# One row-block pair of the q and k projection computed with seven block products instead of eight

## The chip, the cores and the metric

The kernel runs on one core of a Trainium2 chip. The metric is the device time of one execution in microseconds (us); the time of a kernel is the median of its runs. Engines by their short names: PE is TensorE (matmuls; PEld its weight loads), DVE is VectorE, ACT is ScalarE, POOL is GpSimd, SP is SyncE, which here only issues DMAs.

## The reference, cut to what matters

One encoder layer of a hybrid model: 256 tokens, 2048 features, all in float32.

```python
hn = rms_norm(h, g_mix_pre[i])
u = hn @ w_in[i]                       # (256, 2048) @ (2048, 5120)
q, k, v, xr, yg = jnp.split(u, [D_ATTN, 2 * D_ATTN, 3 * D_ATTN, 3 * D_ATTN + D_REC], axis=-1)
attn = neighborhood_attention(q, k, v, rpb[i])
rec = rglru_bidirectional(xr, ...) * jax.nn.gelu(yg)
mixed = jnp.concatenate([rms_norm(attn, ...), rms_norm(rec, ...)], axis=-1) @ w_out[i]
h = h + rms_norm(mixed, g_mix_post[i])
...                                    # SwiGLU feed-forward network, then a gated embedding
```

The change is in `u = hn @ w_in`, the first large product. What follows it is the same work in both kernels.

## The kernel before

**Products.** Every large product is 256 tokens times a weight matrix. Weights come in tiles of 512 KB: two row blocks of 128 (a *row-block pair*) by 512 columns, f32. ACT rounds a tile to fp32r (`wh`, line 700), DVE takes the rest (`wl = w - wh`, line 716), and the features are split the same way (`hT_hi`, `hT_lo`, lines 331 and 333). A block product of 128 tokens by 128 rows by 512 columns is then three matmuls of 128x512: hi by hi, lo by hi, hi by lo. The third is the one that reads `wl`. A tile takes two token halves times two row blocks times three, 12 matmuls (`products`, line 758).

**Input projection.** The 5120 columns are ten chunks of 512, in the order `x0 v0 q0 k0 x1 q1 k1 v1 g0 g1`; each chunk has eight row-block pairs. The first two chunks take turns (`turns(first, hT, KS, apart=2)`): x0 and v0 alternate for six pairs, then x0 takes its last two, then v0. This stretch is the *head*; its sixteen tiles are called T0 to T15 here in the order in which PE takes them, so T8 is x0's fifth pair and T9 v0's fifth. From q0 on each chunk runs alone. During the head SP also fetches the transposed input `xs` (two halves of 1 MB; the last load of the second half is behind T9's) and, for the row norms, the input again as four loads `xn` of 512 KB, whose squares ACT sums. Only when these are there (`rstd_x`) can any chunk of the projection leave PSUM.

**A unit of seven.** The feed-forward part already uses, for some row-block pairs, a scheme of 2x2 blocks with seven products instead of eight: the two token halves by two row blocks on one side, the two row blocks by two column chunks on the other. Per pair it needs four sums of feature blocks (`sums_of`, S1, S2, S7, S4), sums of weight blocks (`sum_stream`: three additions of 128x512 on DVE, and one more that a DMA on POOL's queue makes by accumulating, `added`), and a combination of the accumulators in PSUM (`made_of_four`) before the rest of the pairs is added on top. PE does it in three steps: `four_products` (12 matmuls on two tiles, into four PSUM banks), later `two_products` (6) and `one_product` (3): 21 matmuls for two tiles instead of 24.

**What sets the order.** The program is built by a planner (`Plan`): each stream of work is a generator that names the engine, a cost and the slots it takes, and the planner fixes one order for each engine. On the chip each engine then takes its instructions in that order and waits for what is missing. Raw weight tiles have four buffers (`wr`), which the lo step (line 716) frees; split tiles four pairs (`wh`, `wl`); PSUM has eight banks, four called `acc` and four called `sm`. SP's loads stand in one order too: a load that waits for a buffer holds those behind it.

Of the kernel before, what the change touches and what calls it, by code (L numbers as in the profile page):

```python
# [44 lines left out]
PLE_KS = (0, 2)  # L45
BEGIN = (6, 7)
# [5 lines left out]
def seven_ks(f):  # L52
# [13 lines left out]
    (lambda c: (("w_ple_gate", c), ("w_ple_gate", c + 1)), (2,), PLE_KS),  # L66
]
# [187 lines left out]
def layer(ctx: ExitStack, tc: tile.TileContext, a: dict, out: bass.AP):  # L255
# [211 lines left out]
    class Group:  # L467
# [23 lines left out]
        def two(self, j):  # L491
            i = len(tiles)
            tiles.append(None)
            self.twos[j] = i
            lower[self.own[j] + 1] = -1
            segs.append((two_products, self, j, i))
# [77 lines left out]
    def load_stream():  # L574
        for i, tl in enumerate(tiles):
# [3 lines left out]
            w, k, n0 = tl  # L579
            if min(fours) <= i < i_ple:  # L580
# [40 lines left out]
    def sum_stream():  # L621

        for i in sorted(fours):
# [26 lines left out]
            done(ev_raw[two, 2])  # L650

# [54 lines left out]
    def lo_stream():  # L706
        last_one = max(f[1] for f in ffn_fours().values())
        for i in range(len(tiles)):
# [16 lines left out]
            if i in fours:  # L725
                plan.add(last_sum(i), plan.now, -2 * SOON)

# [74 lines left out]
    def made_of_four(group):  # L802
# [49 lines left out]
    def sums_of(lhs, kx, hi, lo):  # L852
# [7 lines left out]
        kind = "mid" if lhs is hP or kx == 6 else "T4"  # L860
        for j in range(2):
            h, l = lhs.at[kx + j]
            yield dve(S, take=None if j else kind)
            if not j and kind == "mid":
# [107 lines left out]
    for i in range(2 * NT):  # L972
        extra_loads.setdefault((10 + i, 0), []).append(load_xn(i))
# [75 lines left out]

    def open_p1():  # L1050
        t1["hs"], t1["rec_hi"] = big(0, "hs", F32), big(1, "rec_hi")
# [14 lines left out]
        for n in ("qh", "ql", "kh", "kl"):  # L1066
            t1[n] = p1.tile([P, HB, S], F32R, name=n)
        for n in ("vh", "vl"):
            t1[n] = p1.tile([P, NT, N], F32R, name=n)
        t1["pp"] = p1.tile([P, 2, NT, 2, KEYS], F32R, name="pp")  # L1070
# [6 lines left out]
        nc.gpsimd.memset(ssr, 0.0)  # L1077

# [20 lines left out]
    def second_tiles():  # L1099
        plan.reach(ev_x)  # L1100
        t1["rec_lo"], t1["attnT"] = big(2, "rec_lo"), big(3, "attnT", F32)
# [393 lines left out]
    first = []  # L1495
    for n, c in enumerate(ORDER.split()):
        (n0, post), half = CHUNKS[c[0]], int(c[1])
        ch = Chunk(post(half), (open_p1, second_tiles)[n] if n < 2 else None)
        if n < 2:
            first.append((ch, "w_in", n0 + half * N))  # L1500
        if n == 1:
            turns(first, hT, KS, apart=2)
        elif n > 1:
            seg(ch, "w_in", n0 + half * N, hT, KS, after=start_biases if n == 3 else None)
# [747 lines left out]
    for i in range(min(fours), max(f[1] for f in fours.values() if f[4] is hF.ev_sums)):  # L2252
        if i % (W_BUFS + MORE_W) < MORE_W:
            more_w[i] = i % (W_BUFS + MORE_W)
    places = list(RING)
    for n, i in enumerate(sorted(lower)):
        lower[i] = next(j for j in places if j < 3 or n < len(lower) - 4)
        places.remove(lower[i])
        places.append(lower[i])
    first_slot = {i: n % 2 for n, i in enumerate(sorted(fours))}  # L2260
# [147 lines left out]
```

## Time and profile before

| | us |
|---|---|
| median of 3 runs (1138.49 to 1139.64) | 1139.56 |
| the profiled execution, its time | 1138.81 |
| the profiled execution, its span | 1137.0 |
| PE busy | 1127.5 |
| DVE busy | 962.1 |
| ACT busy | 741.0 |
| POOL busy | 154.5 |

The span runs from the first to the last instruction; 1.81 us of the execution lie around it. Busy time of PE is of little use as a share: a matmul of 128x512 is booked with 390 ns, while the next starts 227 ns after it. What counts is whether PE ever waits, and that is read from the rows of its waits and from the starts of its weight loads. In the page's forty slices PE's granted clock stands at 9 (90% or more) throughout. The DMA engines move 237 GB/s on average over the span.

### The profile page before, as it was taken

The numbers are of one execution on the slowest core, as the hardware profiler recorded it, in microseconds if no ns is written. First come the engines' busy times: TensorE is split into PE (matmuls) and PEld (weight loads), VectorE is DVE, ScalarE is ACT, GpSimd is POOL, SyncE is SP. The second block draws the span as 40 slices with busy tenths as digits, with TensorE's granted clock in tenths as the row PEclk, the third lists the DMA queues.
The fourth block names the chain that finished last, engine by engine and source line by source line (L and its number), as shares of the span: only waits on it lengthen the run. The fifth ranks groups of instructions, "written<-read, shape, count | busy, mean of one in ns | idle before, by whom it ended". The sixth has DMA issues, their size and how long they took to land.

```text
span 1137.0 us, 15223 instructions
## 1 busy us (share of the span) xinstructions
PE 1127.5 (99%) x5140; PEld 938.2 (83%) x5140; DVE 962.1 (85%) x1250; ACT 741.0 (65%) x994; POOL 154.5 (14%) x245
## 2 busy tenths in 40 slices
PE   9999999999999999999999999999999999999997
PEld 8888888888888888888888888888888888888886
DVE  6768787788469998899998889999989988888986
ACT  6776788876448566566566656666565664676674
POOL 0000000000000032232011043132121223200200
PEclk9999999999999999999999999999999999999999
DMA  8867566565686986887887777897887788967862
GB/s 311 303 193 219 173 183 187 166 201 181 206 302 184 344 254 226 234 259 222 277 285 232 240 222 216 249 269 235 271 275 280 233 242 255 305 208 271 269 198 101
DMA packets 110686, 269.54 MB, mean 237 GB/s; under 512 B 36432, under 2 KB 42576, under 8 KB 109200
## 3 DMA queue, kind: packets, MB, share of 16 engines
q1 hardware_dynamic: 95568, 242.60, 64.0%
q0 software_dynamic: 14752, 25.84, 11.1%
q8 instruction: 40, 0.66, 0.2%
q14 instruction: 38, 0.31, 0.1%
q10 hardware_dynamic: 288, 0.14, 0.0%
HBM read 250.70 MB, written 9.44 MB: 229 GB/s over the span
## 4 chain that ended last, share of the span: by engine, by line
PE 96%; DVE 1%; ACT 1%; DMA 1%; issue 0%; SPq 0%; DVEq 0%; POOL 0%; ACTq 0%; POOLq 0%
PE acc L758 69%; PE acc L769 8%; PE acc L768 8%; PE acc L767 8%; PE tr L344 1%; DVE wl L716 0%; DMA sq<-ev 0%; PE half L2119 0%; PE acc L2119 0%; PE warm L2305 0%; PE pg L391 0%; PE pg L392 0%; PE pg L393 0%; ACT wh L700 0%; PE po L1435 0%
## 5 line engine op out<-in xcount | busy, mean ns | idle before, releaser
L716 DVE TENSOR_TENSOR wl<-wr,wh 128x1024 fp32r<-128x1024 f32 (+1 forms) x295 | 352.9, 1210 | 77.8 <-ACT wh L700 72.4
L700 ACT CAST wh<-wr 128x1024 fp32r<-128x1024 f32 (+1 forms) x295 | 304.9, 1042 | 136.8 <-PE acc L758 84.2
L758 PE MATMUL acc<-wh,hT_mix_hi 128*128 128x512 f32 x376 | 146.6, 390 | 0.0
L758 PE MATMUL acc<-wh,hT_mix_lo 128*128 128x512 f32 x376 | 146.3, 389 | 0.0
L758 PE MATMUL acc<-wl,hT_mix_hi 128*128 128x512 f32 x376 | 146.3, 389 | 0.0
L700 ACT CAST wh<-ple 128x1024 fp32r<-128x1024 f32 (+1 forms) x75 | 76.0, 1018 | 82.2 <-DVE ple L643 54.6
L363 POOL DMA_DIRECT2D mT<-mid x164 | 96.8, 636 | 238.3 <-DVE mid L353 117.6
L758 PE MATMUL acc<-wl,hT_hi 128*128 128x512 f32 x320 | 124.6, 390 | 0.0
L758 PE MATMUL acc<-wh,hT_hi 128*128 128x512 f32 x316 | 124.5, 394 | 0.0
L758 PE MATMUL acc<-wh,hT_lo 128*128 128x512 f32 x316 | 123.2, 390 | 0.0
L669 POOL DMA_DIRECT2D ple<-in_w_ffn_up x32 | 28.7, 897 | 539.7 <-DVE ple L643 386.3
L716 DVE TENSOR_TENSOR wl<-ple,wh 128x1024 fp32r<-128x1024 f32 (+1 forms) x75 | 88.0, 1177 | 9.3 <-ACT wh L700 9.3
L758 PEld LDWEIGHTS acc<-wl,hT_mix_hi 128*128 128x128 f32 x376 | 70.6, 188 | 14.7 <-DVE wl L716 0.2
L758 PEld LDWEIGHTS acc<-wh,hT_mix_hi 128*128 128x128 f32 x376 | 70.6, 188 | 14.6
L758 PEld LDWEIGHTS acc<-wh,hT_mix_lo 128*128 128x128 f32 x376 | 70.6, 188 | 14.6
L758 PEld LDWEIGHTS acc<-wl,hT_hi 128*128 128x128 f32 x320 | 60.1, 188 | 13.1 <-DVE wl L716 0.2
L758 PEld LDWEIGHTS acc<-wh,hT_lo 128*128 128x128 f32 x316 | 59.4, 188 | 11.6
L758 PEld LDWEIGHTS acc<-wh,hT_hi 128*128 128x128 f32 x316 | 59.4, 188 | 11.4
L758 PE MATMUL acc<-w,hT_mix_hi 128*128 128x512 f32 x144 | 47.3, 389 | 0.0
L716 DVE TENSOR_TENSOR wl<-lower,wh 128x1024 fp32r<-128x1024 f32 x35 | 42.4, 1215 | 3.1 <-ACT wh L700 3.1
L700 ACT CAST wh<-lower 128x1024 fp32r<-128x1024 f32 x35 | 36.6, 1052 | 10.7 <-PE acc L758 6.8
L758 PE MATMUL acc<-wh,hT_ffn_hi 128*128 128x512 f32 x96 | 37.8, 393 | 0.4 <-ACT hT_ffn_hi L331 0.4
(472 smaller groups left out, 2536.6 us busy)
## 6 DMA issues: line engine op xcount, KB each, us to landing
wr<-in_w_in SPq DMA_DIRECT2D x77, 512.0 KB, 4.5
wr<-in_w_ffn_gate SPq DMA_DIRECT2D x70, 512.0 KB, 5.6
wr<-in_w_ffn_down SPq DMA_DIRECT2D x54, 512.0 KB, 6.0
wr<-in_w_ffn_up SPq DMA_DIRECT2D x50, 512.0 KB, 5.0
wr<-in_w_out SPq DMA_DIRECT2D x32, 512.0 KB, 4.4
wr<-in_w_ple_gate SPq DMA_DIRECT2D x30, 512.0 KB, 4.7
lower<-in_w_ffn_up SPq DMA_DIRECT2D x27, 512.0 KB, 6.4
third<-in_w_ffn_gate SPq DMA_DIRECT2D x18, 512.0 KB, 5.7
```

Source lines behind the costliest of these rows:

```text
L344: nc.tensor.transpose(tr[:, b, t * P : (t + 1) * P], e[:, t, sl], ident)
L363: (nc.gpsimd if i in pool else nc.sync).dma_start(dst[32 * j : 32 * j + 32, :, :, i, :], src[32 * i : 32 * i + 32, :, :, j, :],)
L669: nc.gpsimd.dma_start(dst, src, accum_op=ALU.add)
L700: nc.scalar.copy(his[i][:, 0 : src.shape[1], :] if n == 2 else his[i][:, j, :], src)
L716: nc.vector.tensor_tensor(out=los[i][:, m, :], in0=src, in1=f32(his[i][:, m, :]), op=ALU.subtract)
L758: nc.tensor.matmul(accs[t], x[:, sl], w[:, j, :], start=st and m == 0, stop=sp and m == 2, **group)
L767: nc.tensor.matmul(dst, x[0], wh, start=start, stop=False, skip_group_check=seeded)
L768: nc.tensor.matmul(dst, x[1], wh, start=False, stop=False, skip_group_check=seeded)
L769: nc.tensor.matmul(dst, x[0], wl, start=False, stop=stop, skip_group_check=seeded)
```

## The change

One unit of seven is put into the input projection: row-block pair 0 of q0 and k0 (`IN_KS = (0,)`). Its `four_products` step is placed inside the head, after five turns of x0 and v0 (`IN_AT = (5,)`), that is between T9 and what was T10. Its two tiles Q and R are loaded there; Q takes a `wr` buffer, R a tile of its own. The `xn` loads move four tiles back (from tiles 10 to 13 to tiles 14 to 17 of the new count). x0 and v0 accumulate in the four `sm` banks, q0 and k0 in the four `acc` banks at the same time. After the head q0 and k0 take turns for two pairs, with `two_products` and `one_product` behind them, and then each its last five pairs alone. The four feature sums of pair 0 and three weight sums are made on DVE in the head, and the accumulators are combined there. The scratch tiles use places whose owners are opened later (`open_v`, `open_qk`). The index that assigns split tiles to a fifth place is shifted by two, so that the parts behind the input projection get the places that they had.

```diff
+IN_KS = (0,)
+IN_AT = (5,)
@@ load_stream
+            if i in in_load:
+                for kb, f in extra_loads.get((i, 0), ()):
+                    yield dma(kb)
+                    f()
+                j, second = in_load[i]
+                yield dma(512, take=None if second else "wr")
+                loaded[i] = in_rows[j] if second else raw_tile(i)
+                nc.sync.dma_start(loaded[i], a[w][n0 // N, k // 2])
+                done(ev_load[i])
+                continue
...
+    def in_sum_stream():
+        for j, i in enumerate(into.own):
+            yield ev_load[i]
+            yield ev_load[i + 1]
+            Q, R, both = loaded.pop(i), loaded.pop(i + 1), in_both[j]
+            yield dve(3 * N)
+            nc.vector.tensor_tensor(out=both[:, 0, :], in0=Q[:, 0, :], in1=Q[:, 1, :], op=ALU.add)
+            nc.vector.tensor_tensor(out=both[:, 1, :], in0=both[:, 0, :], in1=R[:, 1, :], op=ALU.add)
+            nc.vector.tensor_tensor(out=Q[:, 1, :], in0=Q[:, 1, :], in1=R[:, 1, :], op=ALU.add)
...
+    def in_last_sum(j):
+        late, last = into.last[j][:2]
+        there = Event()
+        yield from added(in_both[j][:, 1, :], late[:, 0, :], there)
+        yield there
+        raws[last] = in_both[j][:, 1:2, :]
+        done(ev_raw[last, 2])
...
@@ made_of_four
-        yield ev_rf
-        yield act(N)
-        u, v = (t2["pool"].tile([P, N], F32, tag="junk", name="u", bufs=2) for _ in range(2))
+        if group.lhs is hT:
+            u, v = (t1["ig"][:, n, :, :].rearrange("p c s -> p (c s)") for n in range(2))
+            yield act(N)
+        else:
...
-        extra_loads.setdefault((10 + i, 0), []).append(load_xn(i))
+        extra_loads.setdefault((14 + i, 0), []).append(load_xn(i))
...
+        ch = Chunk(post(half), {0: open_hs, 1: open_v, 2: open_qk, 3: second_tiles}.get(n), slot="sm" if n < 2 else "acc")
...
-            turns(first, hT, KS, apart=2)
+        if n == 3:
+            into = Group([made_of[m] for m in ORDER.split()[2:4]], hT, KS, IN_KS, apart=5)
+            into.own, into.twos, into.last = [], {}, {}
+            m = len(KS) - 2
+            for i, k in enumerate(KS[:m]):
+                for j, b in enumerate(IN_AT):
+                    if i == b:
+                        into.four(j)
+                for d, w, o in first:
+                    seg(d, w, o, hT, [k], i == 0, False)
...
+            steps = list(('0', 'a'))
+            m = len(into.rest) - into.apart
+            for i in range(m):
+                into.pair(i)
...
+                for x in steps.pop(0) if steps else "":
+                    if x.isdigit():
+                        into.two(int(x))
+                    else:
+                        into.one(range("abc".index(x), "abc".index(x) + 1))
...
+    plan.add(in_sums(), 17.0, late=-LATE)
+    plan.add(in_sum_stream(), late=-LATE)
```

**DVE in the head.** First the order before, from the lo steps of T5 to T7 (`wl`, the first row) up to the lo steps of T10 to T13 (the last); `hT_lo` with `xs_82` is the lo part of the features' second half.

```order
L716 TENSOR_TENSOR wl<-wr,wh 128x1024 x3
L333 SCALAR_TENSOR_TENSOR hT_lo<-xs_82,g_first,hT_hi 128x256 x4
L716 TENSOR_TENSOR wl<-wr,wh 128x1024
L333 SCALAR_TENSOR_TENSOR hT_lo<-xs_82,g_first,hT_hi 128x256 x4
L716 TENSOR_TENSOR wl<-wr,wh 128x1024 x4
```

Now the changed order at the same place, from the lo step of T6; `here` holds the feature sums, `at_lo` their lo part, `both_kl` two of the weight sums.

```order
L766 TENSOR_TENSOR wl<-wr,wh 128x1024
L927 TENSOR_TENSOR here<-hT_hi,hT_lo 128x256
L336 SCALAR_TENSOR_TENSOR hT_lo<-xs_82,g_first,hT_hi 128x256 x4
L766 TENSOR_TENSOR wl<-wr,wh 128x1024
L934 TENSOR_TENSOR here<-here 128x128 x4
L336 SCALAR_TENSOR_TENSOR hT_lo<-xs_82,g_first,hT_hi 128x256 x4
L766 TENSOR_TENSOR wl<-wr,wh 128x1024
L330 TENSOR_TENSOR at_lo<-here,at_hi 128x512
L673 TENSOR_TENSOR both_kl<-wr 128x512
L674 TENSOR_TENSOR both_kl<-both_kl,rows_qh 128x512
L675 TENSOR_TENSOR wr<-wr,rows_qh 128x512
L766 TENSOR_TENSOR wl<-wr,wh 128x1024
```

T7's lo step now stands behind the first four `hT_lo` instead of ahead of them, T8's behind the second four, and T9's (the last row) behind T8's and four instructions of the new unit.

**ACT in the head.** Before, from the casts of T6 and T7 (first row) to that of T11 (last row):

```order
L700 CAST wh<-wr 128x1024 x2
L331 ACTIVATE hT_hi<-xs_82,g_first 128x256 x2
L700 CAST wh<-wr 128x1024
L331 ACTIVATE hT_hi<-xs_82,g_first 128x256 x2
L700 CAST wh<-wr 128x1024
L331 ACTIVATE hT_hi<-xs_82,g_first 128x256 x4
L995 ACTIVATE xn_83,ss_x<-xn_83 128x1024
L700 CAST wh<-wr 128x1024
L995 ACTIVATE xn_83,ss_x<-xn_83 128x1024
L700 CAST wh<-wr 128x1024
```

And in the changed kernel from the second four `hT_hi` on; `ig<-acc_437` and `acc_438<-ig` are the two copies of `made_of_four`, and the cast behind the second of them is x0's seventh pair, called T14 (Q and R are T10 and T11 in the new count).

```order
L334 ACTIVATE hT_hi<-xs_82,g_first 128x256 x4
L328 CAST at_hi<-here 128x512
L750 CAST wh<-both_kl 128x1024
L1069 ACTIVATE la_149<-vec 128x16
L750 CAST wh<-wr 128x1024 x2
L1053 ACTIVATE xn_83,ss_x<-xn_83 128x1024
L750 CAST wh<-wr 128x1024
L1071 ACTIVATE la_149<-la_149 128x16
L872 COPY ig<-acc_437 128x512
L1053 ACTIVATE xn_83,ss_x<-xn_83 128x1024
L862 COPY acc_438<-ig 128x512
L750 CAST wh<-wr 128x1024
```

T14's cast stands behind the second `xn` square sum and behind both copies.

**SP in the head.** Before, from T8's load (`wr_272`) to T12's (`wr_374`):

```order
L612 DMA wr_272<-in_w_in 128x1024
L971 DMA vec_69<-in_vecs 128x152
L612 DMA wr_285<-in_w_in 128x1024
L957 DMA xs1_82<-in_xT 128x1024
L965 DMA xn0_83<-in_x 128x1024
L612 DMA wr_318<-in_w_in 128x1024
L965 DMA xn0_83<-in_x 128x1024
L612 DMA wr_354<-in_w_in 128x1024
L965 DMA xn1_84<-in_x 128x1024
L612 DMA wr_374<-in_w_in 128x1024
```

In the changed kernel, from T9's load (`wr_319`) to T14's (`wr_417`); `wr_345` is Q and `rows_qh` is R.

```order
L626 DMA wr_319<-in_w_in 128x1024
L1015 DMA xs1_82<-in_xT 128x1024
L591 DMA wr_345<-in_w_in 128x1024
L591 DMA rows_qh_140<-in_w_in 128x1024
L626 DMA wr_374<-in_w_in 128x1024
L626 DMA wr_397<-in_w_in 128x1024
L1023 DMA xn0_83<-in_x 128x1024
L626 DMA wr_417<-in_w_in 128x1024
```

Up to the last `xs` load the two orders are the same; behind it Q and R stand where the first `xn` and T10 stood, and the `xn` loads follow later.

## Rows read from the trace of the kernel before

**Rows 1.** The page: busy us, share of the span and instructions by engine.

```profile
PE 1127.5 (99%) x5140; PEld 938.2 (83%) x5140; DVE 962.1 (85%) x1250; ACT 741.0 (65%) x994; POOL 154.5 (14%) x245
```

**Rows 2.** Waits of PEld, whole span: us in total, times, longest.

```profile
PEld final L2206 <- ACT diag L2204: 2.9, 1, 2.9
...
PEld sc L391 <- DVE pp L327: 0.5, 1, 0.5
PEld acc L758 <- DVE wl L716: 0.3, 2, 0.2
```

**Rows 3.** Timeline of PEld: start, duration, instruction, idle before and releaser.

```profile
17.06 0.19 PEld L758 LDWEIGHTS acc<-wl,hT_hi 128*128 128x128 f32 x1 [0.15 <-DVE wl L716]
...
27.86 0.19 PEld L758 LDWEIGHTS acc<-wl,hT_hi 128*128 128x128 f32 x1
...
30.58 0.19 PEld L758 LDWEIGHTS acc<-wl,hT_hi 128*128 128x128 f32 x1
```

**Rows 4.** Timeline of DVE in the head.

```profile
15.79 1.22 DVE L716 TENSOR_TENSOR wl<-wr,wh 128x1024 fp32r<-128x1024 f32 x1
...
17.72 2.35 DVE L716 TENSOR_TENSOR wl<-wr,wh 128x1024 fp32r<-128x1024 f32 x2
...
25.00 1.22 DVE L716 TENSOR_TENSOR wl<-wr,wh 128x1024 fp32r<-128x1024 f32 x1
26.49 1.69 DVE L333 SCALAR_TENSOR_TENSOR hT_lo<-xs,g_first,hT_hi 128x256 fp32r<-128x256 f32 x4 [0.27 <-ACT hT_hi L331]
28.09 1.22 DVE L716 TENSOR_TENSOR wl<-wr,wh 128x1024 fp32r<-128x1024 f32 x1
```

**Rows 5.** Timeline of ACT in the head.

```profile
21.32 0.91 ACT L331 ACTIVATE hT_hi<-xs,g_first 128x256 fp32r<-128x256 f32 x2
...
25.95 1.71 ACT L331 ACTIVATE hT_hi<-xs,g_first 128x256 fp32r<-128x256 f32 x4 [0.28 <-DMA xs<-in_xT]
28.67 1.06 ACT L995 ACTIVATE xn<-xn 128x1024 f32<-128x1024 f32 x1 [1.01 <-DMA xn<-in_x]
...
30.04 1.05 ACT L700 CAST wh<-wr 128x1024 fp32r<-128x1024 f32 x1 [0.22 <-DMA wr<-in_w_in]
```

**Rows 6.** Timeline of SP's queue in the head.

```profile
19.38 0.42 SPq L957 DMA_DIRECT2D xs<-in_xT  x1
```

**Rows 7.** DVE at a unit of seven of the feed-forward part.

```profile
383.14 0.69 DVE L327 TENSOR_TENSOR s<-ple,s 128x512 fp32r<-128x512 f32 x1 [0.29 <-ACT s L325]
383.75 0.68 DVE L641 TENSOR_TENSOR ple<-wr 128x512 f32<-128x512 f32 x1
384.47 0.69 DVE L643 TENSOR_TENSOR ple<-ple,lower 128x512 f32<-128x512 f32 x1
385.08 0.69 DVE L647 TENSOR_TENSOR wr<-wr,lower 128x512 f32<-128x512 f32 x1
```

**Rows 8.** DVE combining the accumulators of that unit (first of four).

```profile
395.72 0.68 DVE L818 TENSOR_TENSOR u<-u,acc 128x512 f32<-128x512 f32 x1
```

**Rows 9.** ACT's two copies for it.

```profile
393.90 0.57 ACT L816 COPY u<-acc 128x512 f32<-128x512 f32 x1
...
397.23 0.59 ACT L810 COPY acc<-u 128x512 f32<-128x512 f32 x1 [1.80 <-DVE u L820]
```

**Rows 10.** Feature sums of the feed-forward part: min/median/max ns, first and last start.

```profile
L869 DVE TENSOR_TENSOR ple<-hT_mix_hi,hT_mix_lo x6: 418/418/427, 363.2 to 378.9; 128x256 f32<-128x256 f32 x6
```

**Rows 11.** DMA issues of the first 70 us: count, KB each, median us to landing.

```profile
xn<-in_x SPq DMA_DIRECT2D x4, 512.0 KB, 10.0
```

**Rows 12.** A stretch near the end: us, busy of PE, PEld, DVE, ACT, POOL, granted clock, DMA share, GB/s.

```profile
1129.00:1131.00 2.00, 0.00 (x0) 0.00 (x0) 1.46 (x6) 1.76 (x4) 0.00 (x0) 1.00 0.03 9
```

**Rows 13.** Timeline of PE at the start.

```profile
1.14 4.21 PE L2305 MATMUL warm<-ones 128*128 128x128 f32 x18 [1.14 <-POOL ones L309]
...
6.00 0.60 PE L742 MATMUL acc<-wh,hT_hi 128*128 128x512 f32 x1
6.43 0.40 PE L743 MATMUL acc<-wh,hT_lo 128*128 128x512 f32 x1
```

More of the change, by code (lines that the diff above doesn't have):

```diff
@@ L494, in two @@
             self.twos[j] = i
-            lower[self.own[j] + 1] = -1
+            if self.lhs is not hT:
+                lower[self.own[j] + 1] = -1
             segs.append((two_products, self, j, i))
@@ L650, in sum_stream, with in_sums @@
             done(ev_raw[two, 2])
+    def in_sum_stream():
[7 more added lines that the diff above has]
+            nc.vector.tensor_tensor(out=Q[:, 1, :], in0=Q[:, 1, :], in1=R[:, 1, :], op=ALU.add)
+            raws[i] = both
+            done(ev_raw[i, 2])
+            raws[i + 1], raws[into.twos[j]] = Q, R
+            done(ev_raw[i + 1, 2])
+            done(ev_raw[into.twos[j], 2])
+    def in_last_sum(j):
[5 more added lines that the diff above has]
+        done(ev_raw[last, 2])
+    def in_sums():
+        more = t1["pool"].tile([P, 2, N], F32R, name="sums_more")
+        pairs = [[x.rearrange("p k s -> p (k s)") for x in at0], (more[:, 0, :], more[:, 1, :])]
+        for n, kx in enumerate(IN_KS):
+            if n == 2:
+                for e in hT.ev[8:]:
+                    yield e
+                pair = big(1, "sums_in").rearrange("p (n m) s -> p n (m s)", m=2)
+                pairs.append((pair[:, 0, :], pair[:, 1, :]))
+            p = pairs[n]
+            yield from sums_of(hT, kx, *p, t1["here"])
     ends_with, ends_in = {}, {}
@@ L726, in lo_stream @@
                 plan.add(last_sum(i), plan.now, -2 * SOON)
+            if i in into.own:
+                plan.add(in_last_sum(into.own.index(i)), plan.now)
     MM = 0.2263
@@ L811, in second @@
             done(there)
-        yield ev_rf
-        yield act(N)
-        u, v = (t2["pool"].tile([P, N], F32, tag="junk", name="u", bufs=2) for _ in range(2))
+        if group.lhs is hT:
+            u, v = (t1["ig"][:, n, :, :].rearrange("p c s -> p (c s)") for n in range(2))
+            yield act(N)
+        else:
+            yield ev_rf
+            yield act(N)
+            u, v = (t2["pool"].tile([P, N], F32, tag="junk", name="u", bufs=2) for _ in range(2))
         nc.scalar.copy(u, q1)
@@ L850, in one_product, with sums_of @@
         spent(i)
-    def sums_of(lhs, kx, hi, lo):
+    def sums_of(lhs, kx, hi, lo, here=None):
         lhs.sums[kx] = {
@@ L859, in sums_of @@
         yield lhs.ev[kx + 1]
-        kind = "mid" if lhs is hP or kx == 6 else "T4"
+        kind = None if here is not None else "mid" if lhs is hP or kx == 6 else "T4"
         for j in range(2):
@@ L863, in sums_of @@
             yield dve(S, take=None if j else kind)
-            if not j and kind == "mid":
+            if not j and not kind:
+                e, f = here[:, 0, :], here[:, 1, :]
+            elif not j and kind == "mid":
                 at_ = mid_tile()
@@ L2259, in layer @@
         places.append(lower[i])
+    in_load = {i + n: (j, n) for j, i in enumerate(into.own) for n in range(2)}
+    for i in in_load:
+        ev_load[i] = Event()
+    for j, i in enumerate(into.own):
+        gives[i] = gives[into.twos[j]] = gives[into.last[j][1]] = "x"
     first_slot = {i: n % 2 for n, i in enumerate(sorted(fours))}
```

51 lines of the change are left out of this document (37 added, 14 removed).

## The prediction

> **What bounds the kernel now.** I read the busy times first, then PE's waits, then the starts of its weight loads. Busy times put PE at 1127.5 of the span's 1137.0 us [rows 1], but a busy share does not show whether PE is held, so the waits decide: in the whole execution the weight loads wait 2.9 us at the very end, 0.5 us once for a bank of the attention, and 0.3 us in two goes for a `wl` [rows 2]. So PE is never held for long, and the kernel takes as long as PE's matmuls stand in a row. Their step is read from the third weight loads of T8 and T9, 27.86 and 30.58 [rows 3]: 12 matmuls take 2.72 us, 0.2267 us each. Two consequences. A matmul that goes is worth 0.2267 us. And any pause that the change opens on PE costs its full length, for nothing later has slack to give it back: there are 0.8 us of inner waits in all [rows 2].
>
> How near to a pause is the head? In T4 the third matmul's weight load stands at 17.06, 0.15 us late, with DVE's `wl` as its releaser [rows 3]; that lo step ran from 15.79 to 17.01 [rows 4]. So a lo step that ends at t lets PE go at t + 0.05. In T8 the lo step ended at 25.00 + 1.22 = 26.22 and the load stood at 27.86: 1.6 us to spare. In T9 it ended at 28.09 + 1.22 = 29.31 against 30.58: 1.2 us to spare [rows 3, 4]. The head lives on a margin of a little over one lo step, and that is where the change puts work.
>
> **What it removes.** Eight block products become seven: 24 matmuls become 21, on the same tiles. 3 x 0.2267 = 0.68 us less on PE. Everything behind the input projection keeps its order on all engines.
>
> **What it adds on DVE, and where.** The unit's instructions and their prices: two additions of 128x256, 0.42 us each [rows 10]; four subtractions of 128x128, each no longer than that; the lo part of the feature sums and three weight sums of 128x512, which in the feed-forward part start 0.61, 0.72 and 0.61 us after each other [rows 7]; four combinations of 128x512. DVE has idle time for them in bulk. What matters is where they stand in its order.
>
> Step 1, T7. ACT's cast of T7 is followed by four `hT_hi` in place of two; two took 0.91 and four 1.71 us, and the first began at 21.32 [rows 5]. The four `hT_lo` at 26.49 ended 0.52 after their `hT_hi` (28.18 against 27.66 [rows 4, 5]). So these four end at about 21.32 + 1.71 + 0.52 = 23.55, and T7's lo step, now behind them, at 23.55 + 1.22 = 24.8. PE wants it 2.72 before T8's, at 25.14. It fits, 0.3 us to spare. The four small subtractions then end by 24.8 + 4 x 0.42 = 26.5 at the latest, under the wait for `hT_hi`. They cost nothing; without that cover they would cost what runs past 26.49.
>
> Step 2, T8. The second four `hT_hi` wait for the last half of `xs`; they began at 25.95 with that DMA as releaser [rows 5], issued at 19.38 [rows 6]. SP's order up to there is unchanged, and what stands behind it in the queue cannot bring it forward, so the four `hT_lo` run at 26.49 as before. T8's lo step, which ran ahead of them, now runs behind them: it takes the place that T9's had, 28.09 to 29.31 [rows 4]. PE gets it at 29.36 and wants it at 27.86. **Pause: 1.50 us.**
>
> Step 3, T9. Behind T8's lo step stand the lo part of the feature sums, the three weight sums and only then T9's lo step. From 28.09: a lo step to the next instruction 1.14 (two took 2.35, less one's 1.22 is 1.13 [rows 4]), then 0.61 + 0.72 + 0.61 + 0.61 [rows 7], so T9's starts at 31.78 and ends at 33.00; PE gets it at 33.05. PE wants it 2.72 after T8's third load, at 29.36 + 2.72 = 32.08. **Pause: 0.97 us.** It needs Q and R by 29.8 and 30.6: before, the first `xn` and T10 stood in those two places of the queue and were there for ACT at 28.67 and 30.04 [rows 5]. They are in time.
>
> Step 4, behind it. Both new lo steps (34.1, 35.3) and T12's (36.4) end before PE wants them (35.8, 37.1, 38.5). PE opens the unit at about 35.3 and its 12 matmuls end at 35.3 + 2.72 + 0.39 = 38.4. The copy takes 0.57 [rows 9], the second copy starts 1.51 after DVE's first subtraction [rows 8, 9] and takes 0.59, a cast takes 1.05 [rows 5], a lo step 1.22: T14's ends at about 43.4, and PE wants it at 33.05 + 4 x 2.72 = 43.9. It fits by half a microsecond. x0's evacuation waits for the four squares, which stand four tiles further back, and PE's transposes of x0 stand inside v0's last tile. I take zero for it; the nearest row of PE waiting at a small product, 0.5 us [rows 2], is its bound upward. The loads need no price: Q and R are loads that came later anyhow, and POOL's accumulating DMA of 256 KB has the whole stretch from T11 to the second pair of q0 and k0.
>
> **Sum.** -0.68 + 1.50 + 0.97 = +1.79 us. On the profiled execution, 1138.81, that is 1140.6; this execution is 0.75 below the median of the three runs, so on the median 1139.56 + 1.79 = **1141.3 us**. Later parts change order too (q0 and k0 end nearer together, scores and softmax of the first heads move back by one chunk's middle), under a planner whose order for before left 0.5 us there [rows 2]; I take zero, and -0.5 to +0.7 as bounds: the one wait gone, or that wait again and a little more.
>
> Here the Trainium skill disagrees with a row. TensorE: Matmul & The Clock Gate, Part 2 (What happens when you issue a matmul), says that PE pulls weight loads ahead of matmuls in flight. In the row at 17.06 the weight load itself stands idle for `wl` although it loads `hT_hi`. By the rule each pause would be shorter by the load's 0.19 us and the sum would be +1.4; by the row it is +1.79, and I go by the row.
>
> **Rivals.**
> *A, the pauses stay away (DVE is ahead of my times).* If the last half of `xs` lands earlier than 25.9, steps 2 and 3 move with it. At 24.4 the first pause is gone and the second stays, since its 3.7 us of DVE work follow from T8's lo step: -0.68 + 0.97 = +0.3, 1139.9. With both gone and the 0.5 us wait too, -1.2, 1138.4. Against it: the same order on SP, and DVE's row for the second four is a fact of that landing. That the change does what it says and pays in full ends here, still under 0.2%.
> *B, slower: the square sums hold up ACT.* In the new order ACT takes the second `xn` square sum between the two copies of the accumulators, and T14's cast stands behind both. ACT takes instructions in turn, so if that load is late everything behind waits. It can be issued only behind T14's load, which waits for the buffer that T9's lo step frees at 33.0, so at about 33.5. Up to a landing at about 39.8 it is covered by DVE's subtractions and T14's half microsecond. At the median of the four `xn` loads before, 10.0 us [rows 11], it lands at 43.5: square sum, copy, cast and lo step then end at 43.5 + 1.06 + 0.59 + 1.05 + 1.22 = 47.4 against 43.9, 3.5 us more: 1144.8. For it: the measured landing. Against it: those loads stood in a full queue (512 KB about every 1.4 us, 28.67 to 30.04 [rows 5]), while here at most three loads are ahead, which is 33.5 + 4 x 1.4 = 39.1.
> *C, PE's clock falls in the pauses.* PE sat idle for the 2 us from 1129 with the granted clock still at 1.00 [rows 12], and my pauses are shorter, with 2.3 us of matmuls between them. If it fell all the same, matmuls would step by 0.43 as at 6.00 and 6.43, a level that lasted from PE's first work at 1.14 until then [rows 13]: 5.3 us at half speed cost 2.65 us more, 1143.9. The Trainium skill, same page, section HAM oscillation, says that PE falls to 1.2 GHz when waits part its bursts of matmuls, and that a kernel can pay for it at each such wait. The row speaks against it for pauses of this size.
>
> **How the numbers follow.** Within 0.2%, which is 2.28 us, a measurement of this kernel hardly tells a change from none. The main case, +1.79 with small additions of either sign (T14, the transposes, the later order), 0.70; of this about a third, 0.24, goes over +2.28, since the two thin margins of step 4 can only add. A 0.17, of which 0.03 for a gain past 2.28 us that no row of mine explains. B 0.09 and C 0.04, both slower. So faster 0.03, same 0.46 + 0.14 = 0.60, slower 0.24 + 0.13 = 0.37. The range takes the main case with its bounds on both sides, a part of A below and the beginning of B above: 1139.1 to 1143.6.
>
> **What would show it.** In the changed profile PE has 3 matmuls fewer. PEld has a wait for `wl` of about 1.5 us near 29 and one of about 1 us near 33; the weight load that opens the unit stands near 35.3. Right in kind but not in size: the waits are there, a few tenths off. Wrong: no wait of PEld before 40 (A), or a longer one near 44 or 53 with an `xn` or `rstd_x` behind it on ACT (B), or matmuls stepping by 0.43 after a pause (C). What would make me wrong beyond that is a new wait between 60 and 300 us, where order changes most and I priced nothing.

## The result

| | before | changed |
|---|---|---|
| median of the runs, us | 1138.50 (11 runs) | 1141.04 (10 runs) |
| lowest and highest | 1137.79 to 1139.64 | 1140.35 to 1142.47 |
| the profiled execution, its time | 1138.81 | 1140.35 |
| the profiled execution, its span | 1137.0 | 1138.6 |
| ratio of the times | | 1.0022, 95% interval 1.0012 to 1.0031 |

An eleventh execution of the changed kernel took 1415.08 us at a granted clock of 0.752 and is left out; with it the median is 1141.17.

The changed kernel takes 0.22% more, about 2.5 us: a small loss, but the interval lies above 1. The median, 1141.04, lies 0.3 us from the forecast 1141.3. That nearness is partly luck. The forecast added +1.79 to a median of three runs, 1139.56; over all eleven runs the kernel before has a median of 1138.50. The difference of the medians is +2.54, that of the two profiled executions +1.54. The sum came near the profile, in part because its errors cancel, as the part on the prediction shows; about a microsecond of the medians was not in it.

The page's busy line of the changed kernel, columns as in [rows 1]: PE has three matmuls fewer, DVE 8.5 us more work.

```profile
PE 1127.0 (99%) x5137; PEld 937.1 (82%) x5137; DVE 970.6 (85%) x1266; ACT 743.4 (65%) x999; POOL 155.4 (14%) x246
```

Waits of PEld in the changed kernel, the whole span, columns as in [rows 2]:

```profile
PEld acc L810 <- DVE wl L766: 3.4, 3, 1.9
PEld final L2307 <- ACT diag L2305: 2.9, 1, 2.9
...
PEld tr L347 <- ACT ev L1186: 0.4, 1, 0.4
...
PEld acc L794 <- ACT wh L750: 0.3, 1, 0.3
```

Against [rows 2]: the wait for `wl` is ten times as long, three waits make it up, there is a new wait at a transpose, and the 0.5 us of the attention's product (`sc` for `pp`) are gone. The wait for `wh` stands at 6.61, in the first tiles. Where the three stand is read from PEld's timeline (28 to 54 us, only the rows that wait):

```profile
29.22 0.19 PEld L810 LDWEIGHTS acc<-wl,hT_hi 128*128 128x128 f32 x1 [1.86 <-DVE wl L766]
...
32.89 0.19 PEld L810 LDWEIGHTS acc<-wl,hT_hi 128*128 128x128 f32 x1 [1.07 <-DVE wl L766]
...
46.84 0.19 PEld L810 LDWEIGHTS acc<-wl,hT_hi 128*128 128x128 f32 x1 [0.43 <-DVE wl L766]
...
53.75 0.31 PEld L347 LDWEIGHTS tr<-ident,ev 128*128 128x128 f32 x3 [0.37 <-ACT ev L1186]
```

These are T8, T9, T15 and x0's transposes. What a wait costs is read from PE's own rows, since a weight load has a little slack ahead of its matmul: in the kernel before, the third load of T8 stands at 27.86 [rows 3] and its matmul 0.22 us behind it:

```profile
27.86 0.39 PE L758 MATMUL acc<-wh,hT_lo 128*128 128x512 f32 x1
28.08 0.39 PE L758 MATMUL acc<-wl,hT_hi 128*128 128x512 f32 x1
```

PE of the changed kernel around T8 and at T9:

```profile
27.40 0.39 PE L810 MATMUL acc<-wh,hT_lo 128*128 128x512 f32 x1
29.23 0.50 PE L810 MATMUL acc<-wl,hT_hi 128*128 128x512 f32 x1 [1.44 <-DVE wl L766]
29.56 0.39 PE L810 MATMUL acc<-wh,hT_hi 128*128 128x512 f32 x1
...
31.86 0.39 PE L810 MATMUL acc<-wh,hT_lo 128*128 128x512 f32 x1
32.89 0.50 PE L810 MATMUL acc<-wl,hT_hi 128*128 128x512 f32 x1 [0.65 <-DVE wl L766]
```

The first step is 1.83 us where 0.227 is due: a **pause of 1.60 us**. The matmul behind it takes 0.50 in place of 0.39 us and the next starts 0.33 later, so each pause costs another 0.11. By the same reading the pause at T9 is 0.81 us, that at T15 0.17, that at x0's transposes 0.37. Why the lo steps came late stands on DVE's timeline:

```profile
22.79 1.22 DVE L766 TENSOR_TENSOR wl<-wr,wh 128x1024 fp32r<-128x1024 f32 x1
23.92 1.01 DVE L934 TENSOR_TENSOR here<-here 128x128 f32<-128x128 f32 x4
26.35 1.69 DVE L336 SCALAR_TENSOR_TENSOR hT_lo<-xs,g_first,hT_hi 128x256 fp32r<-128x256 f32 x4 [1.41 <-ACT hT_hi L334]
27.95 1.22 DVE L766 TENSOR_TENSOR wl<-wr,wh 128x1024 fp32r<-128x1024 f32 x1
29.09 0.69 DVE L330 TENSOR_TENSOR at_lo<-here,at_hi 128x512 fp32r<-128x512 f32 x1
29.69 0.69 DVE L673 TENSOR_TENSOR both_kl<-wr 128x512 f32<-128x512 f32 x1
...
31.62 1.22 DVE L766 TENSOR_TENSOR wl<-wr,wh 128x1024 fp32r<-128x1024 f32 x1
```

DVE stands idle for 1.41 us ahead of the second four `hT_lo` while T8's lo step, which could have run there, waits behind them. In the kernel before it ran in that hole [rows 4].

The profiles add up. Changed: three matmuls, -0.68; pauses 1.60 + 0.81 + 0.17 + 0.37 and 4 x 0.11 behind them, +3.39; the attention's wait gone with its 0.11, -0.60; PE's first matmuls came out of the lower clock [rows 13] sooner in this execution, so PE stood 0.46 us earlier in T8 (27.40 where the same matmul of the kernel before stands at 27.86), and the first pause is longer by as much, -0.46. Sum +1.65, measured +1.54.

### The profile page after: what moved, and what is told of

The parts are those of the page before. It is cut to its first block, busy times and chain, and to the rows that moved or that the text cites. A ratio compares the mean times of both kernels' runs of the same rounds, so it can differ in the third digit from the quotient of the medians.

```text
span 1138.6 us, 15261 instructions
## 1 busy us (share of the span) xinstructions
PE 1127.0 (99%) x5137; PEld 937.1 (82%) x5137; DVE 970.6 (85%) x1266; ACT 743.4 (65%) x999; POOL 155.4 (14%) x246
## 4 chain that ended last, share of the span: by engine, by line
PE 95%; DMA 2%; DVE 1%; ACT 1%; issue 0%; SPq 0%; DVEq 0%
PE acc L810 68%; PE acc L820 8%; PE acc L821 8%; PE acc L819 8%; DMA xs<-in_xT 1%; PE tr L347 1%; DMA xn<-in_x 1%; DVE wl L766 0%; DMA wr<-in_w_in 0%; PE half L2220 0%; PE acc L2220 0%; PE pg L394 0%; ACT wh L750 0%; PE pg L395 0%; PE pg L396 0%
## 5 line engine op out<-in xcount | busy, mean ns | idle before, releaser
L810 PE MATMUL acc<-wl,hT_hi 128*128 128x512 f32 x312 | 121.8, 391 | 2.1 <-DVE wl L766 2.1
L810 PE MATMUL acc<-wh,hT_hi 128*128 128x512 f32 x308 | 121.4, 394 | 0.0
L810 PE MATMUL acc<-wh,hT_lo 128*128 128x512 f32 x308 | 120.1, 390 | 0.0
```

Of the source, the lines that this page charges most:

```text
L810: nc.tensor.matmul(accs[t], x[:, sl], w[:, j, :], start=st and m == 0, stop=sp and m == 2, **group)
```

## The experiments

All kernels were timed beside the kernel before, in four groups with its medians at 1138.52, 1138.45, 1138.42 and 1138.77. "Over before" is the difference to the median of the group. The theories: **O**, the loss is DVE's order at T8 and T9; **L**, it is the landing of `xs`; **U**, the unit brings it with it elsewhere; **F**, a load further on sets a floor.

### The changed kernel once more

> The changed kernel itself, in another execution. Theory O (order): the loss is the two places in DVE's order, T8's lo step behind the second four hT_lo and T9's behind at_lo and the three weight sums. Then both pauses of PE are there again, 1.6 and 0.8 us as in the first profile, each within 0.3, and the time is 1.5 to 2.6 us over the kernel before. Theory L (landing): the pauses hang on when the last half of xs lands and differ between executions; since the median of the runs (+2.6) is a microsecond more than the profiled execution (+1.5), the two pauses together should then be 3 us or more in a profile near the median. Theory U (unit): a good part of the loss lies elsewhere, in what the unit brings with it (its products, its places in PSUM, the later order); then waits of PE behind 40 us come to over 1 us.

Measured: 1141.48, 2.96 over before, ratio 1.0026 (1.0017 to 1.0035). PEld's waits in this profile (24 to 54 us):

```profile
29.08 0.19 PEld L810 LDWEIGHTS acc<-wl,hT_hi 128*128 128x128 f32 x1 [1.19 <-DVE wl L766]
32.75 0.19 PEld L810 LDWEIGHTS acc<-wl,hT_hi 128*128 128x128 f32 x1 [1.08 <-DVE wl L766]
46.87 0.19 PEld L810 LDWEIGHTS acc<-wl,hT_hi 128*128 128x128 f32 x1 [0.64 <-DVE wl L766]
```

The four waits are there again; as pauses they are 0.93, 0.81, 0.38 and 0.32. The end of the first is the same to 0.14 us (29.22 and 29.08) although PE's first matmuls took half a microsecond longer: T8's lo step ends when it ends, and a later PE loses less. Behind 54 us this profile has one more step late, 0.16 us at 474. No theory was met in full. O had the first pause at 1.6 within 0.3, and the time at 1.5 to 2.6 over; it was 0.93, and 2.96. L had 3 us at T8 and T9 for a profile near the median; this one, at 1140.79, is 0.7 under it. U had 1 us behind 40 us, and there were 0.38 + 0.32 + 0.16.

### Moving the unit, or T8, through the planner

Two edits, one by one and together:

```diff
-IN_AT = (5,)
+IN_AT = (6,)
```
```diff
@@ make_hT
                 yield ev_xs[b]
+                if k >= 6:
+                    yield ev_lo[8, 2]
```

> The changed kernel with one difference in DVE's order: T8's lo step and at_lo stand ahead of the second four hT_lo, and so T9's lo step ahead of the weight sums. No work is taken away. Theory O: T8's lo step needs only its cast and runs at about 24.9 to 26.1, while PE wants it at 27.6; T9's ends at about 29.6 and PE wants it at 30.3. Both pauses go, at most 0.3 us is left in the head, and the time is 2.1 to 2.4 us under the changed kernel, that is within 0.5 us of the kernel before. Theory L: xs lands when it lands and the second four hT_lo now end 0.5 to 1 us later, so PE's pause moves to the first product that reads the second half of the features; 1 us or more of the gain does not come. Theory U: the pauses go, but waits of PE behind 40 us take their place, and the time falls by less than 1 us.

> The changed kernel with its unit one turn later (after six turns of x0 and v0 instead of five). In DVE's order T8's lo step still stands behind the second four hT_lo, but T9's and those of the next two tiles now stand ahead of the weight sums. Theory O: the first pause stays (1.6 us, within 0.3), the second goes (0.8 to 0 us), so the time lies about 0.8 us under the changed kernel and 0.7 to 1.8 over the kernel before. Theory L: neither place matters by itself, and both pauses stay or go together. Theory U: the unit's copies and squares now stand nearer the end of the head, so x0's evacuation and its transposes wait longer, 0.5 us or more over the 0.4 us of the changed kernel.

> Both differences at once: the unit one turn later, and T8's lo step and at_lo ahead of the second four hT_lo. Theory O: no pause of PE in the head; what is left is the three matmuls that go (-0.68 us) and the wait of the attention's product that went (-0.5): 0.5 to 1.2 us under the kernel before, about 3 us under the changed kernel. Theory U: the time stays within 0.5 us of the kernel before or above it, with new waits behind 40 us of 0.7 us or more. Theory L: the head keeps a pause of 0.5 us or more at the first product that reads the second half of the features.

Measured: 1149.31, 1142.58 and 1141.64, that is 10.8, 4.1 and 3.1 over before. All three expectations missed, and the reason is the planner. Each edit changes what it reckons with in time, and it then orders what stands behind differently. In the first kernel the pauses at T8 and T9 are gone as O said, but waits stand from 34 us on; PEld, whole span:

```profile
PEld acc L810 <- DVE wl L766: 4.6, 2, 2.5
PEld final L2309 <- ACT diag L2307: 2.9, 1, 2.9
PEld acc L810 <- ACT ev L1188: 2.3, 2, 1.5
PEld tr L347 <- issue: 1.7, 2, 1.5
```

With the unit one turn later, the pause at T9 went as expected, but the lo steps of x0's last tiles now stood behind the combination of the accumulators (a pause of 1.84 us at 49.18). So these three decide little between the theories. They were replaced by kernels in which the planner plans as in the changed kernel and only single instructions are written out at another place.

### Single exchanges

Both hooks call the lo step of one tile ahead of an instruction of DVE; `lo_stream` then leaves it out. All other instructions of all engines and queues keep their order.

```diff
+    def lo_first(i):
+        if i not in written:
+            written.add(i)
+            lo_step(i, slice(0, 2), raws[i])
@@ gained_split, as make_hT calls it for the second four
         yield dve(S, give=give)
+        if first is not None:
+            lo_first(first)
@@ in_sum_stream
             yield dve(3 * N)
+            lo_first(9)
```

The first hook (with T8) is one kernel, the second (T9) another, both the third. The fourth adds an exchange on ACT:

```diff
@@ norm_x
             yield act(DA)
+            if i == 2:
+                hi_first(15)
```

> The changed kernel with one exchange in DVE's order and nothing else moved on any engine or queue: T8's lo step ahead of the second four hT_lo. Theory O (order): T8's lo step then runs at 24.9 to 26.1, under the wait for hT_hi, and the first pause (1.60 us in the first profile) is gone. T9 is wanted by PE 2.72 after T8, at 30.3, and its lo step, still behind at_lo and the three weight sums, ends at about 31.7: the second pause grows from 0.8 to 1.4 us. So 1.0 us is gained of the 2.4 us of pauses, and the time is 1.0 us under the changed kernel. Theory F (floor): in the changed kernel T15's cast stands on ACT behind the third xn square sum, whose load landed at 43.4, and T15's lo step ended just when PE came (a wait of 0.2 to 0.4 us at 46.8). If that landing stays where it is, a PE that comes 1.0 us earlier waits 1.0 us longer there, and the time does not change.

> The changed kernel with one exchange in DVE's order and nothing else moved: T9's lo step ahead of the three weight sums (behind at_lo as before). Theory O: the first pause stays at 1.6 us (or what the landing of xs makes of it), the second, 0.8 us, goes; the weight sums end 1.1 us later, and PE waits at most 0.2 us at the unit. The time is 0.6 to 0.8 us under the changed kernel. Theory F: PE waits 0.8 us longer at T15, near 46.8, and the time does not change.

> Both exchanges, nothing else moved. Theory O: no pause at T8 and T9; the unit's first wl is ready at about 33.4 and wanted at 33.0, so 0.4 us is left there; the time is about 2.0 us under the changed kernel and 0.5 to 1.0 over the kernel before (what is left of the landing's and the start's spread aside). Theory F: PE stands 1 to 2 us longer at T14 and T15, between 41 and 47, and the time falls by less than 0.6 us.

> Both exchanges on DVE, and one on ACT: T15's cast ahead of the third xn square sum instead of behind it. Theory O: the wait at T15 was a minor one; this kernel is at most 0.4 us under the one with both exchanges alone. Theory F: T15's cast no longer waits for the xn load; of what PE lost at T15 in the kernel with both exchanges at least 0.8 us comes back, and what is left stands at T14 or at x0's evacuation near 53.

| exchange | median | over before | ratio (interval) |
|---|---|---|---|
| none (repeated above) | 1141.48 | 2.96 | 1.0026 (1.0017 to 1.0035) |
| T8 | 1140.21 | 1.76 | 1.0014 (1.0006 to 1.0023) |
| T9 | 1139.88 | 1.43 | 1.0015 (1.0006 to 1.0024) |
| T8 and T9 | 1138.83 | 0.38 | 1.0005 (0.9996 to 1.0014) |
| T8, T9, T15's cast | 1138.95 | 0.50 | 1.0008 (1.0000 to 1.0017) |

The waits that were left, PEld, 24 to 50 us. T8 alone:

```profile
31.97 0.19 PEld L823 LDWEIGHTS acc<-wl,hT_hi 128*128 128x128 f32 x1 [1.37 <-DVE wl L761]
46.03 0.19 PEld L823 LDWEIGHTS acc<-wl,hT_hi 128*128 128x128 f32 x1 [0.57 <-DVE wl L761]
```

T8 and T9:

```profile
33.09 0.19 PEld L833 LDWEIGHTS acc<-wh,at_hi 128*128 128x128 f32 x1 [0.21 <-ACT wh L753]
34.35 0.19 PEld L835 LDWEIGHTS acc<-wl,at_hi 128*128 128x128 f32 x1 [0.96 <-DVE wl L762]
42.60 0.19 PEld L824 LDWEIGHTS acc<-wl,hT_hi 128*128 128x128 f32 x1 [0.17 <-DVE wl L762]
```

With T8 put right the first pause is gone and the second grows from 0.81 to 1.11: DVE's work ahead of T9 is the same, and PE now comes earlier. With both, 0.70 us is left at the unit's first `wl`. So **O holds**: two exchanged places in DVE's order, with no work taken away, give back 2.2 to 2.6 us and bring the changed kernel level with the kernel before. The intervals of none and of both lie apart; those of the single exchanges overlap with that of none. T8 alone gave 1.2 us where 1.0 was expected, T9 alone 1.5 where 0.6 to 0.8 was expected: in that profile, the fastest of its eleven runs, T9's wait is gone, the one at T15 too, and the one at x0's transposes fell to 0.25 us. Something of U stays: three matmuls and the attention's wait are gone, 0.68 + 0.60 us, and still the kernel with the two places put right is level and not under; in its profile PE waits at the unit's first `wl` and at x0's transposes. **F falls for these kernels**: the wait at T15 did not grow when PE came earlier, for the third `xn` load is issued behind buffers that the lo steps free, and came earlier too (its square sum started at 41.71 in place of 43.44 us); and the exchange on ACT brought nothing.

### The order alone, in the kernel before

```diff
@@ lo_stream
+                if i == 8:
+                    held.append((los[i], src, his[i]))
@@ make_hT, behind the last of the second four
+                if len(last_four) == 4 and held:
+                    lo, src, hi = held.pop()
+                    nc.vector.tensor_tensor(out=lo, in0=src, in1=f32(hi), op=ALU.subtract)
```

> The kernel before, without the unit and with its own layout, with one exchange in DVE's order: T8's lo step behind the second four hT_lo instead of ahead of them. It is the first of the two orders that the change brings, alone. Theory O (order): the second four hT_lo end at about 28.1, T8's lo step at about 29.3, PE wants it at 27.9: a pause of 1.0 to 1.6 us there (PE started 0.7 us later in the kernel before than in the first profile of the changed one, and a later PE loses less), none at T9, none later; the time rises by as much. Rival (unit): the pause at T8 needs the unit's own work around it (the feature sums, the tiles Q and R in the queue); then less than 0.5 us.

Measured: 1140.50, 2.08 over before, ratio 1.0017 (1.0008 to 1.0025). The order alone, without any unit, costs this much: O again, though the pause in the profile, 1.98 us, is over the 1.0 to 1.6 expected. The profiled execution was the slowest of its eleven, 1142.36, and shows something new. Stretches of it (us, busy of PE, PEld, DVE, ACT, POOL, granted clock, DMA share, GB/s):

```profile
28.00:30.00 2.00, 0.33 (x2) 0.00 (x0) 2.00 (x4) 2.00 (x5) 0.00 (x0) 1.00 1.03 420
30.00:32.00 2.00, 1.85 (x5) 1.49 (x6) 2.00 (x3) 1.68 (x4) 0.00 (x0) 0.65 0.91 301
32.00:34.00 2.00, 2.00 (x6) 1.55 (x5) 1.32 (x2) 1.99 (x3) 0.00 (x0) 0.50 0.99 393
34.00:36.00 2.00, 2.00 (x10) 1.64 (x10) 0.69 (x2) 1.67 (x4) 0.00 (x0) 0.99 0.98 367
```

PE's rows there:

```profile
27.94 0.39 PE L763 MATMUL acc<-wh,hT_lo 128*128 128x512 f32 x1
30.15 0.50 PE L763 MATMUL acc<-wl,hT_hi 128*128 128x512 f32 x1 [1.82 <-DVE wl L994]
30.48 0.51 PE L763 MATMUL acc<-wh,hT_hi 128*128 128x512 f32 x1
30.79 0.63 PE L763 MATMUL acc<-wh,hT_lo 128*128 128x512 f32 x1
31.21 0.63 PE L763 MATMUL acc<-wl,hT_hi 128*128 128x512 f32 x1
...
33.77 0.51 PE L763 MATMUL acc<-wl,hT_hi 128*128 128x512 f32 x1
34.12 0.40 PE L763 MATMUL acc<-wh,hT_hi 128*128 128x512 f32 x1
```

A pause of 1.98 us, and then matmuls step by 0.43: the granted clock is 0.50, the lower of the two levels (1.2 GHz), until about 34. From 30.48 to 34.12 nine steps take 3.64 us where 2.04 is due: 1.60 us on top of the pause. This is rival C of the prediction, in a kernel where the pause is a little longer.

### The last load of xs earlier

```diff
@@ the loads ahead of T9's tile
         nc.sync.dma_start(vec, a["vecs"])
+        nc.sync.dma_start(xs_half[1][:, 4:8, :], a["xT"][:, 12:16, :])
```

> The changed kernel with one exchange in SP's queue: the last load of xs ahead of T9's tile instead of behind it, issued at about 17.4 instead of 18.9 us. DVE's order is the changed one. Theory L (landing): the first pause is set by that load, since the second four hT_hi had waited for it (0.3 us in the first profile); it lands 1 us or more earlier, the hT_hi and hT_lo with it, and the first pause falls from 0.9 to 1.6 us to 0.6 or less; the time is 0.8 us or more under the changed kernel. Theory O: ACT's cast ahead of the hT_hi starts only when PE lets go of a split tile, at 24.45, and ends at 25.4, so the hT_hi start at most 0.4 us earlier; the first pause falls by 0.4 at most, the second stays at 0.8, and T9's tile, which now lands later, costs nothing; the time is 0 to 0.4 us under the changed kernel.

Measured: 1141.86, 3.4 over before, not faster than the changed kernel. Both were wrong; L in sign. ACT, 25 to 28 us:

```profile
25.56 1.05 ACT L750 CAST wh<-wr 128x1024 fp32r<-128x1024 f32 x1 [2.85 <-DMA wr<-in_w_in]
26.51 1.70 ACT L334 ACTIVATE hT_hi<-xs,g_first 128x256 fp32r<-128x256 f32 x4
```

T9's tile, now behind `xs` in the queue, lands later; its cast, ahead of the `hT_hi`, starts at 25.56 instead of 24.45, and these start at 26.51 instead of 25.80. In the changed kernel the DMA engines were busy for all of that stretch (share 1.02 and 406 GB/s from 24 to 26 us), so here a load that went ahead of another only traded places with it. The pause was 2.12 us, and here too the clock fell behind it (0.50 from 32 to 34 us).

### Two attempts to get under the kernel before

Both keep the two exchanges and put `at_lo` behind the weight sums, so that the cast of the unit's first tile comes 0.6 us earlier. The first also puts the table load and the root of the row norms ahead of T18's cast, the second T15's cast ahead of the third `xn` square sum.

```diff
@@ split, as sums_of calls it for the unit
+        if behind is not None:
+            behind.append((lo, src, hi))
+            return
@@ in_sum_stream, behind the third sum
+            lo, src, hi = behind.pop()
+            nc.vector.tensor_tensor(out=lo, in0=src, in1=f32(hi), op=ALU.subtract)
```

> The changed kernel with T8's lo step ahead of the second four hT_lo and T9's ahead of the weight sums, and two more exchanges: at_lo behind the three weight sums, so that these run 0.6 us earlier and the cast of the unit's first tile with them, and on ACT the table load and the root of the row norms ahead of T18's cast, so that x0's evacuation starts about 0.9 us earlier. Theory O: of the 0.7 us that PE still waited at the unit's first wl (34.4) at most 0.2 is left, of the 0.35 us at x0's transposes (52.3) nothing; with the three matmuls less the time is 0.5 to 1.0 us under the kernel before. Rival: what is left of the waits moves on, to T14's lo step behind the accumulators' combination or into the attention part, and the time stays within 0.3 us of the kernel with the two exchanges alone, that is 0.1 to 0.7 over the kernel before.

> The changed kernel with four exchanges and nothing else moved: T8's lo step ahead of the second four hT_lo, T9's ahead of the weight sums, at_lo behind the weight sums, and on ACT T15's cast ahead of the third xn square sum. Theory O: no wait of 0.2 us or more in the head up to x0's transposes (52.3, 0.3 us stay); with three matmuls less and without the attention's wait of 0.5 us the time is 0.3 to 0.9 us under the kernel before. Theory V (the later order has a thin place of its own): the square of x1's evacuation waits for a transfer near 136 us, which in the profiles so far cost PE nothing five times and 0.7 to 1.0 us four times; then the median stays within 0.4 us of the kernel before, whatever the head gains, and a profile that shows this wait is 0.7 us or more above one that does not.

Measured: 1139.19 (ratio 1.0003, 0.9994 to 1.0012) and 1139.13 (1.0002, 0.9993 to 1.0011): level with the kernel before, not under it. The wait at the unit's first `wl` is gone in the first and 0.31 us of PEld in the second, but the next ones show: a pause of 0.70 us at T15 in the first, whose cast stands behind the third square sum (ACT waits 1.80 us for that load, until 42.50); T15 in order and 0.70 us at the tile behind it in the second, whose cast stands behind the fourth square sum. So F, which fell above, is met once PE comes earlier still: a load sets the next floor. x0's transposes still waited 0.3 to 0.4 us; in the first kernel T18's cast, put behind the root, still stood ahead of the evacuation, which my expectation had overlooked. And both profiles have a pause of 1.04 us near 139 us. ACT there in the second kernel (133 to 141 us):

```profile
136.95 0.69 ACT L1220 ACTIVATE ev<-acc,rstd_x 128x512 f32<-128x512 f32 x1 [2.45 <-DMA sq<-ev]
```

And in the kernel with T8, T9 and T15's cast, which had no such pause:

```profile
135.44 0.69 ACT L1213 ACTIVATE ev<-acc,rstd_x 128x512 f32<-128x512 f32 x1 [1.27 <-DMA sq<-ev]
```

x1's evacuation waits until a transfer has read the buffer that it is to fill, and that wait ends 1.5 us apart in the two profiles. In the order of the kernel before, no evacuation stands there. Theory V says that this place takes the head's gain away in some executions: the three profiles of exchanged kernels with this pause (0.75 to 1.04 us) took 1139.93, 1140.51 and 1140.40 us, at the upper end of their runs, the two without it or any other late pause 1138.89 and 1138.74. These are five profiles of different kernels and no edit of that place: V fits them and is not shown.

## Why the prediction was right, point by point

The mechanism was right: T8's and T9's lo steps come late in DVE's order, PE pays in full, and the two exchanges take the loss away. The size was near for a weaker reason. At the times that PE had before, the two pauses cost 1.26 and 0.92 us with the 0.11 behind each, where the sum had 1.50 and 0.97; T15 and x0's transposes cost 0.28 and 0.48 where it had nothing, and the attention's wait gave 0.60 back where it had nothing. These errors of up to 0.6 us nearly cancel.

- **No long wait of PE before**: not quite. The view of [rows 2] also has, in rows that I passed over, 0.6 us for `hT_ffn_hi` and three waits of 0.2 to 0.3 us, so the inner waits are 2.1 us and not 0.8. The 0.6 stands in the changed kernel as it was, and the sum does not suffer.
- **-0.68 for three matmuls**: right, 5137 in place of 5140.
- **Step 1, T7 fits**: right with more room. Its lo step ended at 24.01; I had 24.8.
- **Step 2, T8**: right in its mechanism. Its lo step ran from 27.95 to 29.17 (I had 28.09 to 29.31), the load stood at 29.22 (29.36). That the pause was 1.60 beside my 1.50 is luck, for PE came 0.46 us early; in a second execution, where it came 0.07 late, the pause was 0.93. I had read the pause from the load, which on time stands 0.22 us ahead of its matmul: that lead is lost without cost to PE, and 0.11 us comes back on the next step. The experiment on the kernel before shows the cause apart from the unit.
- **Step 3, T9**: right. 31.62 to 32.84 (31.78 to 33.00), load at 32.89 (33.05), pause 0.81 (0.97). The durations taken from the feed-forward unit [rows 7] held in the head: the first weight sums start 0.72 and 0.61 apart there too.
- **Step 4**: T14 fitted, as said; its lo step ended at 42.5, PE wanted it at 43.7. What I did not look at was the tile behind it. T15's cast stands behind the third `xn` square sum:

```profile
43.44 1.06 ACT L1053 ACTIVATE xn<-xn 128x1024 f32<-128x1024 f32 x1 [2.16 <-DMA xn<-in_x]
44.40 0.18 ACT L1053 ACTIVATION_READ_ACCUMULATOR xn<-xn 128x1 f32 x1
44.49 1.03 ACT L750 CAST wh<-wr 128x1024 fp32r<-128x1024 f32 x1
```

  That is rival B's mechanism, one tile later and small: 0.17 and 0.38 us. At the second square sum, where I had put it, the load landed at 38.46, before the 39.8 up to which it was covered.
- **x0's transposes at zero**: wrong by 0.37 and 0.32 us, inside the bound of 0.5 that I had set.
- **The later order at zero, -0.5 to +0.7**: in the first profile the lower end, the 0.5 us gone. In other executions of kernels with this later order, 0.16 to 0.78 us stood at 474 us and 0.75 to 1.04 near 139 (the latter in no profile of the changed kernel itself). I had named a new wait between 60 and 300 us as what would make me wrong, and priced it at nothing.
- **The size of the sum**: +1.79 against +1.5 and +2.0 in the two profiles, and +2.54 in the medians. What the medians have over the profiles is not shown: the thin places at 139 and 474, a first pause that differs between executions (0.93 and 1.60 us here), or a fall of the clock (worth 1.60 us in the run on the kernel before) could make it up, but no execution of the changed kernel above its median was profiled.
- **The weight load**: the sum went by the row in which the load itself waits, and the row holds: at 29.22 the load of `hT_hi` stands idle with the `wl` as its releaser, and its matmul starts with it. In size the trace lies between the two sums: the load is 1.81 us late and PE loses 1.60 + 0.11, which is 0.1 less, where the forecast took nothing off and the other sum 0.19. The Trainium skill (TensorE: Matmul & The Clock Gate, Part 2, What happens when you issue a matmul) says that PE pulls weight loads ahead of matmuls in flight: the trace agrees for a load on time, 0.22 us ahead of its matmul, and not for one whose matmul waits for `wl`.
- **Rival C**: not in the two profiles of the changed kernel (the clock stays at 1.00 behind 1.60 us), but the row I held against it, an idle PE at clock 1.00 near the end [rows 12], was no evidence. In the run on the kernel before, the clock is still 1.00 all through the pause and falls only behind it, once PE runs again. At 1129 I stopped reading too soon: PE takes its last two small products from 1131.17 on, and from 1133 the clock of the kernel before stands at 0.50:

```profile
1133.00:1134.00 1.00, 0.00 (x0) 0.00 (x0) 0.18 (x1) 0.00 (x0) 0.00 (x0) 0.50 1.03 363
```

  So the chance of 0.04 rested on a row that could not bear it; a pause of 1.98 us cost the clock, and what one of 1.50 does in other executions is not shown. The Trainium skill (TensorE: Matmul & The Clock Gate, section HAM oscillation) says that waits between bursts of matmuls can bring PE to the lower clock. Four of the runs agree, listed in the last section.

Not tried: what the layout of the tiles costs without the unit, and why the attention's wait of 0.5 us went.

## What to carry to other kernels

A step that waits for a load should not stand ahead of one that could run meanwhile, on an engine that takes its instructions in turn: the hole of 1.41 us ahead of it is paid by whoever needs the next instruction. To test an order that a planner makes, move one instruction behind the planner's back; an edit to its rules moves everything else too, here by up to 8 us. And when one wait is priced, price the same step of the tiles behind it: of four late places in the head I had found two.

## What was not expected of the hardware

- **The clock at the longest pauses.** Pauses of PE of 0.7 to 1.86 us in these runs were followed by matmuls at the full clock; pauses of 1.98, 2.12, 2.23 and 3.49 us went with a stretch at 0.50, which cost 1.60 us in the one worked out. Whether the length alone decides is not shown. In the first three PE had resumed when the clock fell, as in the rows above; in the longest it fell just before (0.50 from 48.8 to 49.2, PE again at 49.29). The stretch of the first kernel of the planner's group (pause of 2.23 us, ended at 42.24), columns as above:

```profile
40.00:42.00 2.00, 0.17 (x1) 0.00 (x0) 2.00 (x3) 0.50 (x2) 0.00 (x0) 1.00 1.03 406
42.00:44.00 2.00, 1.76 (x6) 1.44 (x7) 1.90 (x6) 1.82 (x3) 0.00 (x0) 0.75 0.98 350
44.00:46.00 2.00, 2.00 (x6) 1.57 (x5) 0.44 (x5) 1.58 (x4) 0.00 (x0) 0.50 0.98 274
```

- **A pause is dearer than its length** by 0.11 us even at the full clock: the matmul behind it takes 0.50 us in place of 0.39, and the next starts 0.33 us after it in place of 0.227 (29.23 and 29.56).
